# Loads behind the moves of turned tiles, mirroring in two steps, and new tables in a two-layer encoder on one core

## The chip, the core and the metric

The kernel runs on one core of a Trainium2 chip. Five engines take part, each with its own instruction stream: TensorE (PE; its weight loads are listed as PEld) multiplies, VectorE (DVE) and ScalarE (ACT) work on tiles, GpSimd (POOL) does a few small things and issues transfers, and SyncE (SP) does nothing but issue transfers. Two queues of transfers matter: that of SP and that of POOL. The metric is the device time of one execution in microseconds (us), the median of several runs.

## What is computed

The reference is a trunk of two layers over 256 positions of width 2048 with 16 heads, all in float32:

```python
# layer 1
u = rms_norm(h, a_norm_g);  q, k, v, fz = split(u @ a_w_in)     # q, k normalized per head
o = forgetting_attention(q, k, v, log_sigmoid(fz + a_b_f))      # causal, with a cumulative bias
h = h + o @ a_w_out
h = h + (relu(rms_norm(h, g) @ w1) ** 2) @ w2                   # w1: 2048 x 8192, w2: 8192 x 2048
# keys and values for layer 2, once
k_sh, v_sh = split(rms_norm(h, kv_norm_g) @ kv_w)               # k_sh normalized per head
# layer 2
q = rms_norm_heads(rms_norm(h, b_norm_g) @ b_w_q)
o = chunked_relbias_attention(q, k_sh, v_sh, b_rel)
h = h + o @ b_w_out
h = h + (relu(rms_norm(h, g) @ w1) ** 2) @ w2
```

## The kernel before

**Split products.** Each float32 operand is split into a high half, rounded, and a low half, what the rounding left. A product of weights and activations takes three passes: high by high (L628), high weights by low activations (L630), low weights by high activations (L632). The high half of a 128x1024 piece of weights is made by ACT (`hi`, L310), the low half by DVE (`lo`, L319), which needs the high one. There are four buffers for high halves and four for low ones. A *unit* is one such piece and its 12 matmuls on 512 columns (six in a form's half, below).

**The feed-forward.** Its hidden width is worked off in four chunks. A chunk has four *pairs* of products: w10 and w11 (two halves of `x @ w1`) and w20 and w21 (two halves of the second product); in layer 1 the query projection follows as pairs q0 and q1. A pair is computed partly by a fast matrix scheme with seven products, the *forms* f0 to f6, each in two halves, and partly plainly: the plain units are called a and b, after the two accumulators that they add to. A form takes sums of weight blocks. Blocks `11` and `12` of a pair are brought into their own tiles (`bring`, L337, on SP). `12` gets block `22` added by a transfer that accumulates (T3, L350, on POOL); `make` adds `11` on DVE (T2, L357); T4 adds the raw block `21`, which form f4 used, on DVE (L348); T1 adds `12` to `11` by an accumulating transfer (L350). f4's and f6's blocks and all plain units come through three raw buffers (`raw`, loads L293 and L295 on SP); one is free again when its low halves, or T4 for `21`, have been made. Between forms, partial sums are combined: `p7` (ACT) and then L673 and L675 on DVE, after which the next form writes on.

**Turned tiles.** Results must be transposed before the next product. DVE transposes blocks of 32x32 (L475, `z`), and 16 transfers of 32 partitions each, called moves (L490), bring them to their place: every other one is SP's, the rest POOL's. Hidden values are then taken by ACT (relu L990, squares L995 and L997) and DVE (low half L1001); rows of x by ACT (L451, L454) and DVE (L455), and sums of them for the forms by L433 to L442.

**The order.** Instructions of PE, DVE, ACT and SP run in the order in which they are written. What is written when is set by tables. ORDER lists the units of each pair (`r` takes a plain unit left over from the pair before). LOOK says by how many units the low halves are written ahead of the matmuls of a unit, MORE how many high halves beyond that. BEHIND tells after which form half's low half, and how many low halves later, a `bring`, `make` or `add` is written. HIDDEN, LONG, SHORT, AGAIN and QUERY deal the steps of turned tiles (transposes, moves, splitting) out over the following units; these steps stand in a list, `fill`, of which `run_fill` takes one item per unit. In `fetch` (L378), which runs ahead of each unit, low halves, high halves and then raw loads are written: loads go on while fewer than EARLY (4) halves are waiting. `flip` (L611) mirrors the mean squares of the rows for the reversed order in which keys and values are computed: a copy of the mirrored identity on DVE (L614), a matmul (L615), and what follows from it.

Of the kernel before, what the change touches and what calls it, by code (L numbers as in the profile page):

```python
# [9 lines left out]
F32 = mybir.dt.float32  # L10
# [5 lines left out]
P = 128  # L16
# [13 lines left out]
EARLY = 4  # L30
MINI = 0
HIDDEN = (
# [4 lines left out]
)  # L37
UA = UN // 512
LONG = (
# [4 lines left out]
)  # L44
SHORT = (
# [4 lines left out]
)  # L50
REL = 384
QUERY = (0, 1, 13, 10, 5, 9, 3)
AGAIN = (0, 0, 1, 3, 4, 4, 7, 5)
ATT = ((8, 14, 18, 18, 10), (8, 8, 12, 12, 9), (8, 13, 18, 18, 10), (8, 8, 12, 12, 8))
BIAS = ((3, 6, 7), (3, 6, 4))
LOOK = {
# [6 lines left out]
}  # L63
MORE = {
# [6 lines left out]
}  # L71
ORDER = {
# [9 lines left out]
}  # L82
BEHIND = {
    "w10": {(0, 0): [(0, 1, "make", 0), (7, 1, "add", "T1", 0)], (0, 1): [(2, 1, "add", "T1", 1), (0, 1, "make", 1)], (1, 1): [(1, 0, "bring", "12", 0), (0, 0, "bring", "12", 1)], (3, 1): [(6, 0, "bring", "11", 0), (6, 0, "bring", "11", 1)], (4, 0): [(1, 1, "add", "T4", 0)], (4, 1): [(0, 1, "add", "T4", 1), (9, 0, "add", "T3", 1)], (6, 0): [(0, 0, "add", "T3", 0)]},
    "w11": {(0, 0): [(0, 1, "make", 0), (7, 1, "add", "T1", 0)], (0, 1): [(2, 1, "add", "T1", 1), (0, 1, "make", 1)], (1, 1): [(1, 0, "bring", "12", 0), (1, 0, "bring", "12", 1)], (3, 1): [(5, 0, "bring", "11", 0)], (4, 0): [(0, 1, "add", "T4", 0)], (4, 1): [(0, 1, "add", "T4", 1), (9, 0, "add", "T3", 1)], (6, 0): [(1, 0, "add", "T3", 0)], (2, 1): [(7, 0, "bring", "11", 1)]},
    "w20": {(0, 0): [(7, 1, "add", "T1", 0), (0, 1, "make", 0)], (0, 1): [(0, 1, "make", 1)], (1, 1): [(0, 0, "bring", "12", 0), (1, 0, "bring", "12", 1), (3, 1, "add", "T1", 1)], (3, 1): [(5, 0, "bring", "11", 0), (2, 0, "bring", "11", 1)], (4, 0): [(2, 1, "add", "T4", 0)], (4, 1): [(0, 1, "add", "T4", 1), (8, 0, "add", "T3", 1)], (6, 0): [(0, 0, "add", "T3", 0)]},
    "w21": {(0, 0): [(0, 1, "make", 0), (6, 1, "add", "T1", 0)], (0, 1): [(0, 1, "make", 1), (0, 1, "add", "T1", 1)], (1, 1): [(2, 0, "bring", "12", 1)], (3, 1): [(5, 0, "bring", "11", 0)], (4, 0): [(1, 1, "add", "T4", 0)], (4, 1): [(0, 1, "add", "T4", 1), (9, 0, "add", "T3", 1), (5, 0, "bring", "11", 1)], (6, 0): [(1, 0, "add", "T3", 0)], (2, 1): [(1, 0, "bring", "12", 0)]},
    "q0": {(0, 0): [(0, 1, "make", 0), (7, 1, "add", "T1", 0)], (0, 1): [(3, 1, "add", "T1", 1), (0, 1, "make", 1)], (1, 1): [(0, 0, "bring", "12", 0), (1, 0, "bring", "12", 1)], (3, 1): [(5, 0, "bring", "11", 0), (3, 0, "bring", "11", 1)], (4, 0): [(1, 1, "add", "T4", 0), (0, 0, "add", "T3", 0)], (4, 1): [(0, 1, "add", "T4", 1), (10, 0, "add", "T3", 1)]},
    "q1": {(0, 0): [(0, 1, "make", 0), (9, 1, "add", "T1", 0)], (0, 1): [(5, 1, "add", "T1", 1), (0, 1, "make", 1)], (1, 1): [(1, 0, "bring", "12", 1)], (3, 1): [(7, 0, "bring", "11", 1), (4, 0, "bring", "11", 0)], (4, 0): [(1, 1, "add", "T4", 0)], (4, 1): [(0, 1, "add", "T4", 1), (9, 0, "add", "T3", 1)], (6, 0): [(0, 0, "add", "T3", 0)], (2, 1): [(1, 0, "bring", "12", 0)]},
}  # L90
SUBS = {"1": (2, 2), "2": (2, 2), "q": (2, 2)}
OPENING = (
    (18, "bring", "12", 0),
    (19, "bring", "12", 1),
    (9, "add", "T3", 0),
    (5, "add", "T3", 1),
    (4, "bring", "11", 0),
    (14, "bring", "11", 1),
)
BIG = 2 * UN  # L100
FORMS = ("11", "T3", "T2", "T1", "21", "T4", "22")
# [14 lines left out]
def trunk(ctx: ExitStack, tc: tile.TileContext, t):  # L116
# [19 lines left out]
    ps_o = pool("ps_o", 2, space=PSUM)  # L136
# [24 lines left out]
    first = sm.tile([P, GH], F32, name="first", bufs=1)  # L161
# [216 lines left out]
    def fetch(ahead=AHEAD, early=EARLY, more=0):  # L378
        while (units or raws or highs) and len(ready) <= ahead:
            low()  # L380
        while (units or raws) and len(ready) + len(highs) <= ahead + more and can_high():
            high()
        while units and sum(r[3] for r in raws) < early:
            load()
        return ready.popleft()

    fill = deque()

    def run_fill():
        if fill:  # L390
            for f in fill.popleft():
                f()
# [178 lines left out]
    class RowStats:  # L571
# [37 lines left out]
            yield  # L609

        def flip(self):  # L611
            pm = ps_o.tile([P, 512], F32, name="pt", tag="po")
            flipper = wk.tile([P, P], F32, name="flipper", tag="wk")
            V.tensor_copy(flipper, ident[:, ::-1])  # L614
            TE.matmul(pm[:, :NB], flipper, self.ms, start=True, stop=True)  # L615
# [369 lines left out]
    def mlp(plan, x, Sx, st, last, query=None):  # L985
# [49 lines left out]
        for it in plan:  # L1035
            p = it.pair
            if isinstance(p, Pair):
                n = it.u if it.kind == "f" else 7
                hl = fetch(LOOK[p.key][n], more=MORE[p.key][n])
            else:  # L1040
                hl = fetch()
            assert it.u < 4 or it.kind == "f" or it.u * 2 < len(p.x or range(99)), (p.stage, p.n, it.u, len(p.x))
            if p.ps is None:
                open_pair(p)
                if not p.prev:
                    for ps in (p.ps[1][0], p.ps[0][1]):
                        TE.matmul(ps, p.x[0][:, 0, :P], hl[0][:, :512], start=True, stop=True)
            if it.kind == "f":
                form_products(p, *hl, it.u, it.s)
            else:  # L1050
                products(p.ps[it.kind], *hl, p.x, it.u, not units and not ready, isinstance(p, Pair))
            if it.kind != "f" or it.s == p.subs - 1:
                run_fill()
                q = {"f4": 0, "f5": 0, "f6": 1}.get(f"f{it.u}") if it.kind == "f" else it.kind
                if q is not None:
                    p.left[q] -= 1
                    if not p.left[q]:
                        for b in range(NB):
                            p.evac[q](b, p.ps[q][b])
# [147 lines left out]
```

## Time and profile before

| | |
|---|---|
| median of three runs | 2105.89 us (2103.67 to 2107.0) |
| the profiled execution | 2103.45 us |
| its span | 2101.7 us |
| matmuls busy (PE) | 2069.0 us, 98% |
| VectorE busy | 1723.8 us, 82% |
| ScalarE busy | 1290.3 us, 61% |
| GpSimd busy | 354.8 us, 17% |
| mean transfer rate | 256 GB/s, 538.89 MB in all |

The profile is of one execution. Busy times of PE have modelled ends, so a matmul of 512 columns is shown as 0.39 us where the next starts after 0.23. In a row of the timeline stand the start, the time, engine, line, operation, tiles and how many are taken together; in brackets the idle time before it and what ended it. The feed-forward of layer 1 lies at about 393 to 1130 us with the query pairs at its end, the keys, values and attention of layer 2 up to about 1430, the feed-forward of layer 2 from there to the end.

### The profile page before, as it was taken

The page shows a single profiled execution, that of the slowest core. Times are in us where ns is not written, and L with a number is a line of the kernel's source. Part 1 is how long each engine was busy: PE and PEld are TensorE (multiplying, and loading weights), DVE is VectorE, ACT ScalarE, POOL GpSimd, SP SyncE. Part 2 cuts the span into 40 slices and gives each one's busy share as a digit, 9 for nine tenths or more (in the row PEclk, how much of TensorE's full clock was granted, in tenths as well). Part 3 has the DMA queues.
Part 4 walks back from the last instruction along what each step waited for, and adds up shares of the span by engine and source line. Part 5 has one row for each costly group of instructions (what it writes and reads, how often), then busy time and mean ns, then how long its engine had stood idle before and what let it go on. Part 6 is the DMA issues. An engine that isn't in the chain of part 4 may idle for free. (4 is left out here: it accounts for less than half of the span.)

```text
span 2101.7 us, 26998 instructions
## 1 busy us (share of the span) xinstructions
PE 2069.0 (98%) x9114; PEld 1696.5 (81%) x9114; DVE 1723.8 (82%) x2003; ACT 1290.3 (61%) x1567; POOL 354.8 (17%) x552
## 2 busy tenths in 40 slices
PE   9999999999999999999999999999999999999999
PEld 7888888787887887887777888887878878878877
DVE  6777676898888889888999576768988998898896
ACT  6544545776667567567777444456765765675674
POOL 1001001231032022022224000022310310220220
PEclk9999999999999999999999999999999999999999
DMA  8777778899898898899886777688997988988884
GB/s 304 242 254 225 238 245 277 259 254 274 258 285 244 250 297 246 264 267 282 251 252 202 260 238 239 226 276 254 265 282 251 271 258 262 286 255 258 267 270 167
DMA packets 160635, 538.89 MB, mean 256 GB/s; under 512 B 42848, under 2 KB 68080, under 8 KB 125680
## 3 DMA queue, kind: packets, MB, share of 16 engines
q1 hardware_dynamic: 129136, 453.78, 60.8%
q0 software_dynamic: 31360, 83.39, 21.4%
q8 instruction: 71, 1.16, 0.2%
q14 instruction: 68, 0.56, 0.1%
HBM read 497.20 MB, written 15.75 MB: 244 GB/s over the span
## 5 line engine op out<-in xcount | busy, mean ns | idle before, releaser
L319 DVE TENSOR_TENSOR lo<-raw,hi 128x1024 fp32r<-128x1024 f32 (+1 forms) x634 | 753.4, 1213 | 149.7 <-ACT hi L310 137.4
L310 ACT ACTIVATE hi<-raw 128x1024 fp32r<-128x1024 f32 (+1 forms) x634 | 651.0, 1052 | 330.0 <-PE acc L630 129.6
L628 PE MATMUL acc<-hi,act 128*128 128x512 f32 x1644 | 456.1, 394 | 5.6 <-ACT hi L310 2.0
L632 PE MATMUL acc<-lo,act 128*128 128x512 f32 x1644 | 449.0, 390 | 1.7 <-DVE lo L319 1.7
L630 PE MATMUL acc<-hi,act 128*128 128x512 f32 x1644 | 448.8, 389 | 0.0
L628 PEld LDWEIGHTS acc<-hi,act 128*128 128x128 f32 x1644 | 306.8, 188 | 71.1 <-ACT hi L310 3.6
L632 PEld LDWEIGHTS acc<-lo,act 128*128 128x128 f32 x1644 | 307.9, 188 | 68.4 <-DVE lo L319 4.3
L630 PEld LDWEIGHTS acc<-hi,act 128*128 128x128 f32 x1644 | 308.5, 188 | 65.2 <-DVE act L421 0.5
L319 DVE TENSOR_TENSOR lo<-w,hi 128x1024 fp32r<-128x1024 f32 x204 | 243.8, 1214 | 18.6 <-ACT hi L310 18.4
L310 ACT ACTIVATE hi<-w 128x1024 fp32r<-128x1024 f32 x204 | 211.3, 1053 | 73.3 <-PE po L630 29.8
L490 POOL DMA_DIRECT2D q<-z x336 | 170.3, 517 | 259.1 <-DVE z L475 95.0
L310 ACT ACTIVATE hi<-wT 128x1024 fp32r<-128x1024 f32 x136 | 140.8, 1054 | 77.4 <-DVE wT L348 48.5
L319 DVE TENSOR_TENSOR lo<-wT,hi 128x1024 fp32r<-128x1024 f32 x136 | 160.3, 1216 | 4.8 <-ACT hi L310 3.7
L628 PE MATMUL s<-hi,act 128*128 128x512 f32 x476 | 136.7, 391 | 4.5 <-ACT hi L310 2.8
L632 PE MATMUL s<-lo,act 128*128 128x512 f32 x476 | 137.0, 392 | 0.6 <-DVE lo L319 0.5
L630 PE MATMUL s<-hi,act 128*128 128x512 f32 x476 | 136.0, 390 | 0.0
L628 PEld LDWEIGHTS s<-hi,act 128*128 128x128 f32 x476 | 89.0, 188 | 25.2 <-ACT hi L310 4.1
L632 PEld LDWEIGHTS s<-lo,act 128*128 128x128 f32 x476 | 88.5, 188 | 22.8 <-DVE lo L319 4.8
L630 PEld LDWEIGHTS s<-hi,act 128*128 128x128 f32 x476 | 88.7, 188 | 19.7 <-DVE act L1001 1.4
L727 POOL TENSOR_TENSOR rn<-vv,mhalf 128x4 f32<-128x4 f32 x32 | 44.4, 1401 | 336.3 <-DVE vv L726 336.2
L350 POOL DMA_DIRECT2D w<-in_f1a x32 | 28.6, 967 | 320.4 <-ACT hi L310 191.2
L357 DVE TENSOR_TENSOR wT<-w,w 128x1024 f32<-128x1024 f32 x68 | 82.7, 1217 | 0.0
(183 smaller groups left out, 2333.4 us busy)
## 6 DMA issues: line engine op xcount, KB each, us to landing
raw<-in_w_in SPq DMA_DIRECT2D x94, 512.0 KB, 5.3
raw<-in_s1a SPq DMA_DIRECT2D x32, 1024.0 KB, 6.8
raw<-in_s2a SPq DMA_DIRECT2D x32, 1024.0 KB, 6.7
raw<-in_w_kv SPq DMA_DIRECT2D x64, 512.0 KB, 5.6
raw<-in_s1b SPq DMA_DIRECT2D x32, 1024.0 KB, 6.7
raw<-in_s2b SPq DMA_DIRECT2D x32, 1024.0 KB, 5.7
raw<-in_w_oa SPq DMA_DIRECT2D x32, 512.0 KB, 5.6
w<-in_f1a SPq DMA_DIRECT2D x16, 1024.0 KB, 6.7
```

The costliest lines, as they stand in the source:

```text
L310: S.activation(hi[:, c], raw[:, c], AF.Copy)
L319: V.tensor_tensor(lo[:, c], raw[:, c], hi[:, c].bitcast(F32), op=ALU.subtract)
L350: G.dma_start(d, p.big[block][:, half(s)], accum_op=ALU.add)
L357: V.tensor_tensor(p.t["T2"][:, half(s)], p.t["T3"][:, half(s)], p.t["11"][:, half(s)], op=ALU.add)
L490: (SY, G)[j % 2].dma_start(d[32 * j : 32 * j + 32, i], z[32 * i : 32 * i + 32, j * n : (j + 1) * n])
L628: TE.matmul(ps, xh, cut(hi, j), start=first, stop=False, **kw)
L630: TE.matmul(ps, xl, cut(hi, j), start=False, stop=False, **kw)
L632: TE.matmul(ps, xh, cut(lo, j), start=False, stop=last, **kw)
L727: G.tensor_tensor(rn, vv, mhalf, op=ALU.pow)
```

## The change

Raw loads are no longer written in `fetch` ahead of a unit's matmuls but in a function of their own, `top_up`, which the loop over the feed-forward's plan calls after the unit's matmuls and its step of `fill`. The loops of the other stages load as before. `flip` yields after the copy and again at its end, and its two parts stand in `fill` two items apart. All tables that set the order have new numbers, with a few rows left as they were.

```diff
@@ tables (a few lines of each)
 HIDDEN = (
     (3, 3, 3, 5, 8, 9, 9, 10, 11, 12),
-    (0, 2, 3, 3, 5, 7, 7, 7, 9, 9),
-    (1, 1, 3, 3, 5, 5, 8, 9),
-    (1, 3, 4, 4, 7, 8, 9, 9),
+    (0, 2, 2, 2, 5, 6, 7, 7, 9, 9),
+    (0, 2, 2, 2, 5, 5, 8, 9),
+    (0, 3, 4, 4, 7, 8, 9, 9),
 )
...
-    (8, 0, 1, 2, 2, 3, 4, 4),
+    (7, 0, 0, 0, 1, 2, 4, 4),
...
-    "q0": (2, 2, 2, 2, 1, 2, 1, 2),
+    "q0": (2, 2, 1, 2, 1, 2, 2, 2),
...
-    "w20": "r f0 r f1 f2 f4 r f3 f5 a r r a b f6 r",
+    "w20": "r f0 f1 r f2 f4 r r f3 f5 a a r r b r f6 r",
...
@@ in fetch
         while (units or raws) and len(ready) + len(highs) <= ahead + more and can_high():
             high()
+        if early:
+            top_up(early)
+        return ready.popleft()
+
+    def top_up(early=EARLY):
         while units and sum(r[3] for r in raws) < early:
             load()
-        return ready.popleft()
@@ flip
         def flip(self):
-            pm = ps_o.tile([P, 512], F32, name="pt", tag="po")
             flipper = wk.tile([P, P], F32, name="flipper", tag="wk")
             V.tensor_copy(flipper, ident[:, ::-1])
+            yield
+            pm = ps_o.tile([P, 512], F32, name="pt", tag="po")
             TE.matmul(pm[:, :NB], flipper, self.ms, start=True, stop=True)
...
             self.flipped = f
+            yield
@@ the loop over the plan, and where flip is put
-                hl = fetch(LOOK[p.key][n], more=MORE[p.key][n])
+                hl = fetch(LOOK[p.key][n], 0, MORE[p.key][n])
...
             if it.kind != "f" or it.s == p.subs - 1:
                 run_fill()
+            top_up()
+            if it.kind != "f" or it.s == p.subs - 1:
                 q = {"f4": 0, "f5": 0, "f6": 1}.get(f"f{it.u}") if it.kind == "f" else it.kind
...
-                    add_fill([[]] * QUERY[6] + [[st2.flip]])
+                    step = steps(st2.flip)
+                    add_fill([[]] * QUERY[6] + [[step], [], [step]])
```

The code after is a few lines longer, so lines move: L475 becomes L479, L490 L494, L673 L679, L675 L681, L1001 L1007. Three places show what the new order does.

SP's queue in the first chunk of layer 1, from pair w21's block `12` (in_f2a, the first w tile) to its block `11` (the second) and the raw load behind it; the raw in_f2a between is form f6's of w20, q<-z are moves of hidden tiles. Before:

```order
L337 DMA w_4168<-in_f2a 128x2048
L295 DMA raw<-in_s2a 128x2048
L490 DMA q<-z 32x256 x2
L295 DMA raw<-in_f2a 128x2048
L490 DMA q<-z 32x256 x6
L337 DMA w_4323<-in_f2a 128x2048
L295 DMA raw<-in_s2a 128x2048
```

After:

```order
L337 DMA w_4176<-in_f2a 128x2048
L295 DMA raw<-in_s2a 128x2048
L494 DMA q<-z 32x256 x4
L295 DMA raw<-in_f2a 128x2048
L337 DMA w_4316<-in_f2a 128x2048
L494 DMA q<-z 32x256 x4
L295 DMA raw<-in_s2a 128x2048
```

Block `11` now stands directly behind f6's raw load, with four moves behind it instead of six in front; two more moves stand ahead of the raw load.

DVE in the same place, from the transposes in pair w20 to the low halves of w21's f2 (w_3963 is w20's block `11`, w_4168 and w_4323 are w21's `12` and `11`, wT_4090 is T2 or T4 of w20, wT_4381 T2 of w21). Before:

```order
L475 STREAM_TRANSPOSE z<-acc 128x4x4x32 x2
L319 TENSOR_TENSOR lo<-wT_4090,hi 128x1024 x2
L319 TENSOR_TENSOR lo<-raw,hi 128x1024 x2
L348 TENSOR_TENSOR wT_4090<-wT_4090,raw 128x1024
L673 TENSOR_TENSOR s<-p_4211,po 128x512
L319 TENSOR_TENSOR lo<-w_3963,hi 128x1024
L348 TENSOR_TENSOR wT_4090<-wT_4090,raw 128x1024
...
L319 TENSOR_TENSOR lo<-w_4168,hi 128x1024 x2
L1001 TENSOR_TENSOR act<-q,act 128x1024
L319 TENSOR_TENSOR lo<-wT_4381,hi 128x1024 x2
```

After (w_3945, w_4176, wT_4086 and wT_4379 are the same tiles):

```order
L319 TENSOR_TENSOR lo<-wT_4086,hi 128x1024 x2
L479 STREAM_TRANSPOSE z<-acc 128x4x4x32 x2
L319 TENSOR_TENSOR lo<-raw,hi 128x1024
L348 TENSOR_TENSOR wT_4086<-wT_4086,raw 128x1024
L319 TENSOR_TENSOR lo<-raw,hi 128x1024
L348 TENSOR_TENSOR wT_4086<-wT_4086,raw 128x1024
L679 TENSOR_TENSOR s<-p_4186,po 128x512
L319 TENSOR_TENSOR lo<-w_3945,hi 128x1024 x2
...
L319 TENSOR_TENSOR lo<-w_4176,hi 128x1024 x2
L319 TENSOR_TENSOR lo<-wT_4379,hi 128x1024 x2
L1007 TENSOR_TENSOR act<-q,act 128x1024
```

The transposes stand behind f2's low halves, both T4 additions ahead of L679 and of f3's low halves, and L1007 behind the low halves of w21's f2.

DVE in the query pair q0, around the partial sum that its form f3 waits for (w_8749 and w_8751 are its block `11`, from which f3's two low halves are made). Before:

```order
L475 STREAM_TRANSPOSE z<-h_91 128x4x4x32
L319 TENSOR_TENSOR lo<-w_8749,hi 128x1024 x2
L673 TENSOR_TENSOR s<-p_8965,po 128x512
L319 TENSOR_TENSOR lo<-raw,hi 128x1024 x2
L348 TENSOR_TENSOR wT_8813<-wT_8813,raw 128x1024 x2
```

After:

```order
L479 STREAM_TRANSPOSE z<-h_91 128x4x4x32
L319 TENSOR_TENSOR lo<-w_8751,hi 128x1024
L679 TENSOR_TENSOR s<-p_8961,po 128x512
L319 TENSOR_TENSOR lo<-w_8751,hi 128x1024
L319 TENSOR_TENSOR lo<-raw,hi 128x1024 x2
L348 TENSOR_TENSOR wT_8809<-wT_8809,raw 128x1024 x2
```

L679 stands one low half earlier than L673 did.

More of the change, by code (lines that the diff above doesn't have):

```diff
@@ L39 @@
 LONG = (
[4 rows of a table removed]
[4 rows of a table added]
 )
 SHORT = (
[4 rows of a table removed]
[4 rows of a table added]
 )
 REL = 384
-QUERY = (0, 1, 13, 10, 5, 9, 3)
-AGAIN = (0, 0, 1, 3, 4, 4, 7, 5)
+QUERY = (0, 1, 13, 11, 9, 10, 3)
+AGAIN = (0, 0, 1, 2, 4, 3, 6, 5)
 ATT = ((8, 14, 18, 18, 10), (8, 8, 12, 12, 9), (8, 13, 18, 18, 10), (8, 8, 12, 12, 8))
-BIAS = ((3, 6, 7), (3, 6, 4))
+BIAS = ((3, 6, 7), (8, 6, 3))
 LOOK = {
[6 rows of a table removed]
[6 rows of a table added]
 }
 MORE = {
[6 rows of a table removed]
[6 rows of a table added]
 }
 ORDER = {
[9 rows of a table removed]
[9 rows of a table added]
 }
 BEHIND = {
[L84 to L89, printed above, removed]
@@ new lines @@
+    "w10": {(0, 0): [(0, 1, "make", 0), (8, 1, "add", "T1", 0)], (0, 1): [(2, 1, "add", "T1", 1), (1, 1, "make", 1)], (1, 1): [(1, 0, "bring", "12", 0), (1, 0, "bring", "12", 1)], (3, 1): [(7, 0, "bring", "11", 0), (4, 0, "bring", "11", 1)], (4, 0): [(0, 1, "add", "T4", 0)], (4, 1): [(0, 1, "add", "T4", 1), (9, 0, "add", "T3", 1)], (5, 0): [(1, 0, "add", "T3", 0)]},
+    "w11": {(0, 0): [(0, 1, "make", 0), (6, 1, "add", "T1", 0)], (0, 1): [(3, 1, "add", "T1", 1), (0, 1, "make", 1), (3, 0, "bring", "12", 0)], (3, 1): [(3, 0, "bring", "11", 0)], (4, 0): [(1, 1, "add", "T4", 0)], (4, 1): [(0, 1, "add", "T4", 1), (7, 0, "add", "T3", 1)], (6, 0): [(1, 0, "add", "T3", 0)], (2, 1): [(7, 0, "bring", "11", 1), (2, 0, "bring", "12", 1)]},
@@ new lines @@
+    "w20": {(0, 0): [(7, 1, "add", "T1", 0), (0, 1, "make", 0)], (0, 1): [(0, 1, "make", 1)], (1, 1): [(1, 0, "bring", "12", 0), (4, 1, "add", "T1", 1), (0, 0, "bring", "12", 1)], (3, 1): [(5, 0, "bring", "11", 0), (1, 0, "bring", "11", 1)], (4, 0): [(0, 1, "add", "T4", 0)], (4, 1): [(0, 1, "add", "T4", 1), (7, 0, "add", "T3", 1)], (6, 0): [(0, 0, "add", "T3", 0)]},
+    "w21": {(0, 0): [(0, 1, "make", 0), (7, 1, "add", "T1", 0)], (0, 1): [(0, 1, "make", 1), (0, 1, "add", "T1", 1)], (3, 1): [(5, 0, "bring", "11", 0)], (4, 0): [(0, 1, "add", "T4", 0)], (4, 1): [(0, 1, "add", "T4", 1), (9, 0, "add", "T3", 1), (5, 0, "bring", "11", 1)], (6, 0): [(0, 0, "add", "T3", 0)], (2, 1): [(0, 0, "bring", "12", 0), (2, 0, "bring", "12", 1)]},
@@ new lines @@
+    "q0": {(0, 0): [(7, 1, "add", "T1", 0), (0, 1, "make", 0)], (0, 1): [(4, 1, "add", "T1", 1), (1, 1, "make", 1)], (1, 1): [(1, 0, "bring", "12", 0), (2, 0, "bring", "12", 1)], (3, 1): [(5, 0, "bring", "11", 0), (3, 0, "bring", "11", 1)], (4, 0): [(1, 1, "add", "T4", 0), (0, 0, "add", "T3", 0)], (4, 1): [(0, 1, "add", "T4", 1), (11, 0, "add", "T3", 1)]},
+    "q1": {(0, 0): [(0, 1, "make", 0), (7, 1, "add", "T1", 0)], (0, 1): [(4, 1, "add", "T1", 1), (1, 1, "make", 1)], (1, 1): [(2, 0, "bring", "12", 1)], (3, 1): [(7, 0, "bring", "11", 1), (3, 0, "bring", "11", 0)], (4, 0): [(1, 1, "add", "T4", 0)], (4, 1): [(0, 1, "add", "T4", 1), (9, 0, "add", "T3", 1)], (6, 0): [(0, 0, "add", "T3", 0)], (2, 1): [(3, 0, "bring", "12", 0)]},
@@ L93 @@
     (18, "bring", "12", 0),
-    (19, "bring", "12", 1),
-    (9, "add", "T3", 0),
-    (5, "add", "T3", 1),
+    (17, "bring", "12", 1),
+    (7, "add", "T3", 0),
+    (11, "add", "T3", 1),
     (4, "bring", "11", 0),
-    (14, "bring", "11", 1),
+    (8, "bring", "11", 1),
 )
```

52 rows, old and new, of tables (LONG, LOOK, MORE, ORDER) are left out of this document.

## The prediction

> **What bounds the kernel now.** First the page: span, then the share of each engine.
>
> ```profile
> span 2101.7 us, 26998 instructions
> ...
> PE 2069.0 (98%) x9114; PEld 1696.5 (81%) x9114; DVE 1723.8 (82%) x2003; ACT 1290.3 (61%) x1567; POOL 354.8 (17%) x552
> ```
>
> TensorE is the bound. Since the change leaves its matmuls as they are, only the gaps between them can be won. Next the windows, which show where the gaps are (the columns after the window are its width, then PE, PEld, DVE, ACT and POOL busy, the granted clock, DMA share and GB/s):
>
> ```profile
> 1000.00:1100.00 100.00, 95.44 (x409) 77.13 (x408) 94.08 (x102) 72.79 (x99) 24.27 (x42) 0.98 0.87 253
> ...
> 1200.00:1400.00 200.00, 200.00 (x916) 167.01 (x915) 138.29 (x238) 94.29 (x158) 18.94 (x27) 1.00 0.74 237
> ```
>
> The attention stages have none; the feed-forward has them. Then the timeline of TensorE in one chunk of layer 1 (chunk 2, pairs w20 and w21):
>
> ```profile
> 824.93 1.07 PE L628 MATMUL po<-hi,act 128*128 128x512 f32 x4
> 825.84 1.07 PE L630 MATMUL po<-hi,act 128*128 128x512 f32 x4
> ...
> 835.07 0.73 PE L632 MATMUL acc<-lo,Sh 128*128 128x512 f32 x2 [0.61 <-DVE lo L319]
> ...
> 838.48 0.73 PE L632 MATMUL acc<-lo,Sh 128*128 128x512 f32 x2 [0.40 <-DVE lo L319]
> ```
>
> Four unstalled matmuls take 825.84 - 824.93 = 0.91 us, 226.5 ns each. Busy times include a modelled end, so I count stalls as width less matmuls times 226.5 ns. Every chunk has the same two places: w20's forms f3, f5 and the two units after them (48 matmuls), and w21's forms f0, f1, f2 (36 matmuls; 60 in the last chunk of a layer, where two other units lie between). First rows and sums over the eight chunks, for w20 and then w21:
>
> ```profile
> 479.07:491.10 12.03, 11.51 (x50) 8.77 (x48) 10.41 (x10) 4.85 (x5) 1.73 (x2) 1.00 0.88 222
> ...
> sum 96.53, PE 92.30 PEld 70.19 DVE 83.61 ACT 41.23 POOL 13.71; mean PE 11.54 PEld 8.77 DVE 10.45 ACT 5.15 POOL 1.71
> ```
>
> ```profile
> 496.54:507.21 10.67, 9.08 (x37) 6.47 (x36) 10.67 (x10) 9.81 (x12) 1.71 (x2) 1.00 0.92 230
> ...
> sum 90.63, PE 82.10 PEld 61.32 DVE 89.88 ACT 80.53 POOL 13.69; mean PE 10.26 PEld 7.67 DVE 11.23 ACT 10.07 POOL 1.71
> ```
>
> w20: 96.53 - 384 x 0.2265 = 9.6 us. w21: 90.63 - 336 x 0.2265 = 14.5 us. Together 24 us in a kernel with, by the page, 2101.7 - 2069.0 = 33 us without a matmul. In both places PE waits for DVE's low halves (lo L319). What DVE itself waits for differs. The same chunk, DVE, then ACT, then the SP queue:
>
> ```profile
> 813.47 1.21 DVE L348 TENSOR_TENSOR wT<-wT,raw 128x1024 f32<-128x1024 f32 x1
> ...
> 824.98 2.36 DVE L319 TENSOR_TENSOR lo<-raw,hi 128x1024 fp32r<-128x1024 f32 x2 [1.59 <-ACT hi L310]
> 829.25 1.23 DVE L319 TENSOR_TENSOR lo<-w,hi 128x1024 fp32r<-128x1024 f32 x1 [1.91 <-ACT hi L310]
> ...
> 836.07 1.22 DVE L1001 TENSOR_TENSOR act<-q,act 128x1024 fp32r<-128x1024 f32 x1
> ```
>
> ```profile
> 823.89 2.01 ACT L310 ACTIVATE hi<-raw 128x1024 fp32r<-128x1024 f32 x2 [4.23 <-DMA raw<-in_f2a]
> ...
> 828.16 2.01 ACT L310 ACTIVATE hi<-w 128x1024 fp32r<-128x1024 f32 x2 [0.31 <-DMA w<-in_f2a]
> ```
>
> ```profile
> 814.76 0.33 SPq L295 DMA_DIRECT2D raw<-in_f2a  x1
> 815.14 4.42 SPq L490 DMA_DIRECT2D q<-z  x6
> 819.73 0.47 SPq L337 DMA_DIRECT2D w<-in_f2a  x1
> ```
>
> At w20 DVE has no wait up to 824.98; it is simply full. At w21 it is late because it idled 1.59 + 1.91 = 3.5 us for two transfers: form f6's raw block, issued at 814.76 right behind the second T4 addition (L348), and w21's block w11, issued at 819.73 behind six moves.
>
> **The change part by part.**
>
> *The w20 to w21 crossing.* On DVE both T4 additions of w20 now stand ahead of L679 (old L673; 0.69 us in its row for q0 below) and of the first low half of f3 (2.36 / 2 = 1.2 us, by the rows above), 1.7 us when instructions overlap a little. The transposes, which now come behind f2's two low halves, may wait, though: they used to start at 804.86, so they would start 2.32 later, at 807.2, and the unit that they read ends now where f2's second half used to start, at 807.47.
>
> ```profile
> 804.86 1.30 DVE L475 STREAM_TRANSPOSE z<-acc 128x512 f32<-128x512 f32 x2
> 806.10 2.32 DVE L319 TENSOR_TENSOR lo<-wT,hi 128x1024 fp32r<-128x1024 f32 x2
> ```
>
> ```profile
> 807.47 0.62 PE L628 MATMUL po<-hi,Sh 128*128 128x512 f32 x2
> ```
>
> With the last matmul's drain that is a wait of 0.3 to 0.5, say 0.4 us, so f6's load goes out about 1.7 - 0.4 = 1.3 us earlier. On SP, w11 now stands ahead of the last four moves; it needs f3's low halves, finished at about 816 (the T4 row's 813.47 and two operations of 1.2), and so goes out some 3.4 us earlier. Whether earlier issue is earlier landing is for the DMA engines to say:
>
> ```profile
> 814.00:816.00 2.00, 1.48 (x7) 0.88 (x7) 1.93 (x3) 1.20 (x2) 1.39 (x2) 1.00 0.46 70
> ...
> 826.00:828.00 2.00, 2.00 (x10) 1.65 (x10) 1.34 (x2) 1.06 (x1) 0.00 (x0) 1.00 1.03 426
> ```
>
> They are half empty when f6 is issued and full later. I credit f6 with all 1.3 us, and w11 with 1.5 of its 3.4 (lower end 0, if the engines hand the whole gain back). DVE then starts w21's low halves 1.3 to 1.6 us earlier. Besides, L1007 (old L1001) moves from ahead of f2's low halves to behind them: 1.14 us more for f2 alone. Stalls of 14.5 / 8 = 1.8 us a chunk meet 1.3 to 1.6 us for f1 and 2.4 to 2.7 for f2; what stays is about 0.3 a chunk, 2.4 in all. Term: -12.1, between 0 and -14.5.
>
> *w20 itself.* The same DVE work stands ahead of f3 and the two units, so the 9.6 us stay; the transposes' wait ends up in it. I take a third of its 0.4 us, 0.15 a chunk: +1.2, between 0 and +3.2. On POOL one T3 accumulation now goes ahead of the eight moves, for which I put nothing: POOL is 17% busy, and the moves' reader, the relu on ACT, now stands two high halves later.
>
> *The query pair q0.* PE, DVE and the granted clock:
>
> ```profile
> 1062.56 0.61 PE L632 MATMUL po<-lo,S 128*128 128x512 f32 x2
> 1066.11 0.83 PE L628 MATMUL po<-hi,S 128*128 128x512 f32 x2 [2.93 <-DVE s L673]
> ...
> 1070.51 0.62 PE L628 MATMUL s<-hi,act 128*128 128x512 f32 x2
> ```
>
> ```profile
> 1063.04 2.31 DVE L319 TENSOR_TENSOR lo<-w,hi 128x1024 fp32r<-128x1024 f32 x2
> 1065.27 0.69 DVE L673 TENSOR_TENSOR s<-p,po 128x512 f32<-128x512 f32 x1
> ```
>
> ```profile
> 1066.00:1070.00 4.00, 3.90 (x10) 3.11 (x11) 4.00 (x4) 3.97 (x10) 4.00 (x8) 0.57 0.88 198
> ```
>
> PE stands from 1063.01 (1062.56 and two matmuls) to 1066.11, 3.1 us, because f3 overwrites what L673 must read and L673 stands behind f3's two low halves. After that the clock is 0.57: twelve matmuls take 1070.51 - 1066.11 = 4.4 instead of 2.7 us, 1.7 more. In the new order L679 stands one low half earlier (2.31 / 2 = 1.15 us), so the stall is 2.0 us. I take the slow clock as gone with it, because the stall of 1.9 us that ends at 1147.01 (below) leaves the clock at 1.00 in the next 3.4 us:
>
> ```profile
> 1147.40:1150.80 3.40, 3.40 (x17) 2.81 (x16) 3.33 (x7) 1.90 (x2) 2.12 (x2) 1.00 0.87 287
> ```
>
> Term: -1.1 - 1.7 = -2.8, between -1.1 and -4.8. The Trainium skill (TensorE: Matmul & The Clock Gate, Part 1: The HAM clock gate) says that the clock halves after an idle window of about 3.4 us. The trace differs a little: here 3.1 us were enough; by the rule 2.0 us cost no clock and the term is -2.8, by a lower limit that the row leaves possible it is -1.1.
>
> *Flip in two steps, and the first K/V group.*
>
> ```profile
> 1129.81 0.35 PE L615 MATMUL pt<-msb,flipper 128*128 128x2 f32 x2 [0.87 <-DVE flipper L614]
> ...
> 1147.01 0.73 PE L628 MATMUL acc<-hi,act 128*128 128x512 f32 x2 [1.66 <-DVE qn L731]
> ```
>
> With two units between copy and matmul, the 0.87 us wait goes: -0.9 (0 if the copy slips as far). At 1147 L455 no longer stands between the first K/V low halves and qn (an operation on 128x1024, as L1001's 1.22 us), but its ACT part now precedes the squares: I take half, -0.6, between +1 and -1.7.
>
> *The openings.* At the start of each feed-forward, f5 waits for a high half that stands behind the splitting of turned x:
>
> ```profile
> 1456.43 0.73 PE L628 MATMUL s<-hi,act 128*128 128x512 f32 x2 [1.56 <-ACT hi L310]
> ```
>
> ```profile
> 1452.64 1.71 ACT L451 ACTIVATE y<-q,gsb 128x256 f32<-128x256 f32 x4 [2.51 <-DMA q<-z]
> ```
>
> The moves that L451 waits for now go out one unit's steps earlier in SHORT's last row, and without a raw load between. The transposes ahead of them come no earlier, so I take a part of the 2.51 us only, 0.55, twice (layers 1 and 2): -1.1, between +2 and -3.
>
> Elsewhere a raw load now stands behind the same unit's moves. I put nothing for that: the next row has raw loads waiting 479 us for a buffer, so most are issued as soon as a buffer is free and are early; the cover is the third raw buffer.
>
> ```profile
> SPq L295 <- DVE lo L319: 478.8, 134, 12.8
> ...
> SPq L490 <- DVE z L475: 52.7, 19, 10.2
> ...
> ACT hi L310 <- DMA raw<-in_f2b: 24.0, 6, 5.7
> ```
>
> Sum: -12.1 + 1.2 - 2.8 - 0.9 - 0.6 - 1.1 = -16.3 us. Against the profiled execution (2103.45 us, span 2101.7 and 1.75 around it) that is 2087.1; it ran 2.4 below the median of 2105.89, so the median comes to 2089.6: 2089.
>
> **The rivals.**
>
> *Moves in front of loads (slower).* A move waits for its transposes (L490's row: 2.8 us on average, 10.2 at most) and takes 4.42 / 6 = 0.74 us to issue, and now raw loads queue behind it. Four moves and an average wait make a load 5.8 us later. ACT's row above has loads that are already late, 24.0 us in six waits. If one load a chunk has only 3.5 us to spare, that is 2.3 x 8 = 18 us, and with the other terms (-4.2) and w21's gain kept the sum is about +2; if it is a load in front of w21, its gain is lost as well: +14, 2120. The middle is 2114. It decides as soon as a load is later than its margin; against it speak the 479 us. The Trainium skill (DMA: Bandwidth & Descriptors, Queues, rings and completion order) speaks for it: each DMA engine takes a ring's descriptors in order, so a load behind moves also starts behind their data. No row here shows the order within a ring.
>
> *Nothing won at w21.* The DMA engines are full from 816 us on, w11 lands as late as before, or DVE, which was full for w20, only shifts its stall from w21 to the units behind it. Then -4.2 us of the other terms stay: 2101.7, at the edge of no change. For it: the share of 1.03. Against: DVE's 3.5 us of idle time are real, and f6's load starts with the engines half empty.
>
> *More than costed.* w20's stall shrinks too, since the new order asks for lead time earlier, and the openings reach their bounds: -16.3 - 9 = 2080.
>
> **Chances.** Forecast 0.60 (its own range 2083 to 2097), loads late 0.14, nothing won 0.14, more won 0.12. The range leaves out the late loads and some of the far end: 2078 to 2106. What this kernel's measurement tells from no change is 0.2%, 4.2 us. Faster: 0.60 + 0.12 + 0.06 of the third case = 0.78; same 0.08; slower 0.14.
>
> **What will show it.** Right: no DVE idle time over 2 us in front of w21's f0, PE without waits of 0.4 us or more in w21's f1 and f2, w20's waits as before; a stall of 2 us in front of q0's f3 and a clock of 1.00 behind it; no wait for the flipper. Wrong: new rows of ACT waiting for raw blocks, above all where eight moves stand together; or a w20 stall that grows by what w21's loses.

## The result and the profile after

The changed kernel takes 2088.43 us (median of four runs, 2085.9 to 2090.83), the kernel before 2106.43 in the runs beside it: a ratio of 0.9917 (95% interval 0.9899 to 0.9935). Forecast were 2089 us and a gain of 0.8%. The profiled execution is one of the longer ones, 2090.83 us; its page:

```profile
span 2089.0 us, 27013 instructions
...
PE 2064.4 (99%) x9114; PEld 1697.4 (81%) x9114; DVE 1724.3 (83%) x2003; ACT 1297.5 (62%) x1567; POOL 354.3 (17%) x552
```

So the span of this execution is 12.7 us shorter than that of the profiled one of before, and by the medians the gain is 18.0. The work of DVE and ACT is nearly the same; waits are fewer. The two places in each chunk, first the windows of w21's f0 to f2 (last row and sum), then w20 (sum; here the windows begin with f4, so 60 matmuls each, because the wait has moved in front of f3):

```profile
2030.07:2043.87 13.80, 13.80 (x61) 11.19 (x60) 12.11 (x12) 9.53 (x12) 1.69 (x2) 1.00 0.71 188
sum 78.61, PE 77.39 PEld 61.58 DVE 65.83 ACT 63.49 POOL 9.98; mean PE 9.67 PEld 7.70 DVE 8.23 ACT 7.94 POOL 1.25
```

```profile
sum 118.49, PE 112.29 PEld 88.85 DVE 118.49 ACT 76.68 POOL 38.40; mean PE 14.04 PEld 11.11 DVE 14.81 ACT 9.59 POOL 4.80
```

w21: 78.61 - 336 x 0.2265 = 2.5 us, 12.0 less than before. w20: 118.49 - 480 x 0.2265 = 9.8 us, against 9.6 before (which the same 60 matmuls a chunk also give there). DVE is busy all the time in these windows (118.49 of 118.49).

The crossing in chunk 2 of layer 1, SP's queue, ACT and DVE:

```profile
810.77 0.33 SPq L295 DMA_DIRECT2D raw<-in_f2a  x1
813.59 0.33 SPq L337 DMA_DIRECT2D w<-in_f2a  x1
813.98 2.93 SPq L494 DMA_DIRECT2D q<-z  x4
819.87 0.33 SPq L295 DMA_DIRECT2D raw<-in_s2a  x1
```

```profile
822.83 1.06 ACT L310 ACTIVATE hi<-w 128x1024 fp32r<-128x1024 f32 x1 [1.73 <-PE s L638]
...
825.59 1.04 ACT L996 ACTIVATE q<-q 128x1024 f32<-128x1024 f32 x1
```

```profile
823.93 1.23 DVE L319 TENSOR_TENSOR lo<-w,hi 128x1024 fp32r<-128x1024 f32 x1 [0.68 <-ACT hi L310]
```

Block 11 goes out directly behind f6's raw load, and DVE waits 0.68 us in front of w21's first low half instead of 1.91. ACT's first high half of it now waits for a buffer that PE frees (L638), not for a transfer. The four moves go out at 813.98, and the relu that needs them, L996, does not wait at all.

In q0 the wait in front of f3 is shorter, but the half clock is still there. PE's timeline, then a window behind the wait:

```profile
1062.11 1.06 PE L634 MATMUL po<-hi,S 128*128 128x512 f32 x2 [1.87 <-DVE s L679]
```

```profile
1062.30:1065.60 3.30, 3.30 (x9) 2.52 (x9) 3.30 (x4) 3.27 (x6) 2.83 (x6) 0.50 0.88 273
```

### The profile page after: what moved, and what is told of

The parts are those of the page before. It is cut to its first block, busy times and chain, and to the rows that moved or that the text cites. A ratio compares the mean times of both kernels' runs of the same rounds, so it can differ in the third digit from the quotient of the medians.

```text
span 2089.0 us, 27013 instructions
## 1 busy us (share of the span) xinstructions
PE 2064.4 (99%) x9114; PEld 1697.4 (81%) x9114; DVE 1724.3 (83%) x2003; ACT 1297.5 (62%) x1567; POOL 354.3 (17%) x552
## 4 chain that ended last, share of the span: by engine, by line
PE 87%; DVE 6%; DMA 3%; issue 2%; ACT 2%; SPq 0%; ACTq 0%; DVEq 0%; POOL 0%
PE acc L634 19%; PE acc L636 19%; PE acc L638 18%; PE po L634 5%; PE po L638 5%; PE po L636 5%; PE s L636 5%; PE s L638 5%; PE s L634 4%; DVE lo L319 3%; ACT hi L310 1%; DMA w<-in_f2a 1%; PE s L792 1%; PE po L823 1%; DVE wT L348 1%
## 5 line engine op out<-in xcount | busy, mean ns | idle before, releaser
L310 ACT ACTIVATE hi<-raw 128x1024 fp32r<-128x1024 f32 (+1 forms) x634 | 655.1, 1053 | 320.3 <-PE acc L636 130.9
L638 PE MATMUL acc<-lo,act 128*128 128x512 f32 x1644 | 449.2, 390 | 1.9 <-DVE lo L319 1.8
L638 PEld LDWEIGHTS acc<-lo,act 128*128 128x128 f32 x1644 | 308.0, 188 | 68.8 <-DVE lo L319 4.7
L310 ACT ACTIVATE hi<-w 128x1024 fp32r<-128x1024 f32 x204 | 211.5, 1055 | 100.1 <-PE po L636 30.6
L494 POOL DMA_DIRECT2D q<-z x336 | 170.3, 519 | 234.3 <-DVE z L479 82.0
L310 ACT ACTIVATE hi<-wT 128x1024 fp32r<-128x1024 f32 x136 | 140.9, 1053 | 54.1 <-DVE wT L348 26.5
L638 PE MATMUL s<-lo,act 128*128 128x512 f32 x476 | 136.1, 390 | 0.6 <-DVE lo L319 0.5
L638 PEld LDWEIGHTS s<-lo,act 128*128 128x128 f32 x476 | 89.0, 188 | 20.9 <-DVE lo L319 2.6
```

The source lines that it names most:

```text
L310: S.activation(hi[:, c], raw[:, c], AF.Copy)
L494: (SY, G)[j % 2].dma_start(d[32 * j : 32 * j + 32, i], z[32 * i : 32 * i + 32, j * n : (j + 1) * n])
L638: TE.matmul(ps, xh, cut(lo, j), start=False, stop=last, **kw)
```

## The experiments

My theory after the result: what stands where around the w20 to w21 crossing (block 11 early, L1007 behind f2) gives most of the gain, and the position of the raw loads as such costs and gives little. The rival: the position of the loads is the cause. "Waits" below are always widths less matmuls times 226.5 ns, in the profiled execution; where the clock is at half, the longer matmuls count in them too (about 1.7 us for each 3.4 us at half).

**1. The changed kernel again.**

> The changed kernel once more, since its four runs came in two pairs, near 2086 and near 2091 us. If the pairs are two outcomes of the free position of the clock's window against the wait in q0 (about 2 us), a profiled execution near 2086 should show a granted clock of 1.00 behind that wait, 1.7 us less there, and other small differences. If the pairs have another cause, the clock dips in both. Either way 2085 to 2091.

2091.3 us, ratio 0.9929 (0.9914 to 0.9944), just above what was expected. w21 waits 0.6 us in all here, w20 9.9. The clock dips to half behind q0's wait here too, with a time of 2088.98. No profiled execution fell near 2086, so what separates the lower runs from the higher ones stays open.

**2. The new tables, with raw loads back ahead of the moves.**

```diff
-                hl = fetch(LOOK[p.key][n], 0, MORE[p.key][n])
+                hl = fetch(LOOK[p.key][n], more=MORE[p.key][n])
...
-            top_up()
-            if it.kind != "f" or it.s == p.subs - 1:
```

> The changed kernel with its raw loads back ahead of the unit's moves; tables and flip new. Theory (tables carry the gain): within 4 us of the changed kernel, 2088 to 2092, w21's waits still under 4 us in all. Rival (loads behind moves carry it): 2098 or more, with w21's waits back.

2107.17 us, ratio 1.0004 (0.9990 to 1.0018): the whole gain is gone, and my theory as it stood with it. Counted from the starts of the matmuls, w21 waits 9.4 us here, against 2.5 and 0.6 in the changed kernel's two profiles, and the openings (f4 to f5) 9.9 against 0.6 and 0.3. The crossing in chunk 2, SP's queue, DVE, ACT and PE:

```profile
818.50 0.33 SPq L337 DMA_DIRECT2D w<-in_f2a  x1
824.77 0.33 SPq L295 DMA_DIRECT2D raw<-in_s2a  x1
825.15 2.41 SPq L494 DMA_DIRECT2D q<-z  x4
```

```profile
816.12 2.35 DVE L319 TENSOR_TENSOR lo<-w,hi 128x1024 fp32r<-128x1024 f32 x2
```

```profile
834.35 1.07 ACT L996 ACTIVATE q<-q 128x1024 f32<-128x1024 f32 x1 [3.73 <-DMA q<-z]
```

```profile
836.41 0.73 PE L634 MATMUL acc<-hi,Sh 128*128 128x512 f32 x2 [0.55 <-ACT hi L310]
```

Block 11 was out at 818.5, 2.4 us behind the start of f3's low halves on DVE (816.12), as in the changed kernel, whose row for these is:

```profile
811.21 2.35 DVE L319 TENSOR_TENSOR lo<-w,hi 128x1024 fp32r<-128x1024 f32 x2
```

But four moves stand behind a raw load that waits for a free buffer: they go out 9.0 us behind that start, where the changed kernel issues them 2.8 us behind it. They land at about 834, 18.0 us behind that start against 14.0 in the changed kernel; L996 waits 3.73 us for them, and the high halves of w21's f1 stand behind L996 on ACT. What ACT waited for moves in all, first here, then in the changed kernel:

```profile
ACT y L455 <- DMA q<-z: 21.2, 8, 4.6
ACT q L996 <- DMA q<-z: 20.9, 8, 3.7
```

```profile
ACT y L455 <- DMA q<-z: 2.6, 4, 1.0
...
ACT q L996 <- DMA q<-z: 0.8, 2, 0.4
```

**3. Pair w20's tables alone, on the kernel before** (its rows of LOOK, MORE, ORDER and BEHIND).

```diff
-    "w20": "r f0 r f1 f2 f4 r f3 f5 a r r a b f6 r",
+    "w20": "r f0 f1 r f2 f4 r r f3 f5 a a r r b r f6 r",
```

> The kernel before with the new LOOK, MORE, ORDER and BEHIND rows of pair w20 alone; loads stay ahead of the moves, flip and all else as before. On SP, w21's block 11 then has two moves instead of six in front, on DVE both T4 additions stand ahead of f3's low halves, and L1001 stands behind w21's f2. Theory (the crossing is won by what stands where in w20): w21's waits fall from 14.5 us to under 3, w20's grow by 0.2 a chunk, so about -11 in all, 2095 +-3. Rival (it is the position of the raw loads that wins): no more than -3, 2103 or more.

2105.28 us, ratio 0.9995 (0.9985 to 1.0005). w21's waits go from 14.5 to 12.3 us only, though block 11 is early and L1001 behind f2. ACT:

```profile
ACT q L990 <- DMA q<-z: 16.0, 6, 3.6
```

Before, this row was:

```profile
ACT q L990 <- DMA q<-z: 1.9, 3, 0.9
```

The wait for block 11 was replaced by one for the moves.

**4. The position of the loads alone, on the kernel before.** The edit is `top_up` and its call, without any table.

> The kernel before with raw loads behind the moves of their unit and nothing else. Two of the six moves ahead of w21's block 11 go ahead of f6's raw load, which waits anyway, so block 11 goes out 1.5 us earlier. Theory: w21's waits shrink by a third to a half, 5 us in all, L1001 is still in front of f2; about 2101 +-4. Rival (position of the loads is the cause of the whole gain): 2092 or less. Rival (loads late behind moves): over 2108, with new waits of ACT for raw blocks.

2104.49 us, ratio 0.9985 (0.9975 to 0.9996). w21 waits 13.9 us, half a us less than before. So neither of these two parts gives more than 2 us by itself; the gain is in the order and the position of the loads together.

**5. Loads ahead of the moves in pair w20 only.**

```diff
-                hl = fetch(LOOK[p.key][n], 0, MORE[p.key][n])
+                hl = fetch(LOOK[p.key][n], EARLY * (p.key == "w20"), MORE[p.key][n])
```

> The changed kernel with raw loads ahead of the moves in pair w20 alone; all engines but SP keep their order. At the crossing, four moves then stand behind a raw load that waits for a free buffer. Theory (a move behind such a load goes out some 10 us later, and ACT's relu L996, which waits for it, holds up the high halves of w21's f1 and f2): w21 waits 1 to 1.5 us a chunk, 6 to 10 us in all. Rival (the position of the loads matters elsewhere only): within 2 us of the changed kernel.

2096.41 us, ratio 0.9955 (0.9938 to 0.9971), that is 5 to 8 us more than the changed kernel's two medians. w21 waits 8.3 us, 5.8 more than in the changed kernel's first profile and 7.7 more than in its second, as expected, and ACT waits for moves again:

```profile
ACT q L996 <- DMA q<-z: 15.2, 5, 3.5
```

**6. Loads ahead of the moves in the opening pair only.** In each layer, one raw load goes ahead of the last two of eight moves on SP; PE, DVE and ACT keep their order.

```diff
-                hl = fetch(LOOK[p.key][n], 0, MORE[p.key][n])
+                hl = fetch(LOOK[p.key][n], EARLY * (not p.prev), MORE[p.key][n])
```

> The changed kernel with raw loads ahead of the moves in the first pair of each feed-forward alone: one raw load goes ahead of the last two of eight moves, twice in the kernel. Theory as before: those two moves wait with the load for a buffer, ACT's splitting of turned x (L455) waits for them, f5's high halves stand behind it: 4 us in layer 1, 5 in layer 2, 9 in all. Rival (two moves are worth 1 to 2 us at most): under 4 in all.

2098.34 us, ratio 0.9968 (0.9956 to 0.9979). The waits from f4 to f5 in the openings are 3.8 and 3.7 us instead of 0.2 and 0.4, so 7 of the expected 9; in layer 1, 1.7 us of it is the half clock that followed the wait. With run 5, this reproduces the loss of run 2: 5 to 8 us from pair w20 and 7 to 10 from the openings, of 16 to 19. The size came out nearly right, but not by the expected way. SP's queue and ACT here, in layer 1:

```profile
395.16 3.68 SPq L494 DMA_DIRECT2D q<-z  x6
398.95 0.52 SPq L295 DMA_DIRECT2D raw<-in_s1a  x1
399.52 1.14 SPq L494 DMA_DIRECT2D q<-z  x2
```

```profile
405.50 1.71 ACT L455 ACTIVATE y<-q,gsb 128x256 f32<-128x256 f32 x4 [3.32 <-DMA q<-z]
```

and in the changed kernel, where all eight moves go first:

```profile
395.17 4.98 SPq L494 DMA_DIRECT2D q<-z  x8
400.26 2.66 SPq L295 DMA_DIRECT2D raw<-in_s1a  x2
```

```profile
403.01 1.71 ACT L455 ACTIVATE y<-q,gsb 128x256 f32<-128x256 f32 x4 [0.83 <-DMA q<-z]
```

The load hardly waits for a buffer, and the two moves are issued only half a us later; yet their reader starts 2.5 us later. One load is 1 MB, and at the 442 GB/s of the next window it is 2.4 us of transfer:

```profile
402.00:403.00 1.00, 1.00 (x6) 0.81 (x6) 1.00 (x2) 0.18 (x1) 0.00 (x0) 1.00 1.04 442
```

So the moves' bytes come behind the load's. The Trainium skill (DMA: Bandwidth & Descriptors, Queues, rings and completion order) has the rule, that each DMA engine consumes the descriptors of one ring in order. SP's two moves fit it in sign and in size. But the rule is about one ring, and the trace shows that the delay isn't bound to SP's queue. POOL's last two moves here were issued just ahead of the load and just behind it, at 398.77 and 399.26:

```profile
L494 POOL DMA_DIRECT2D q<-z x2: 496/497/498, 398.8 to 399.3; - x2
DMA to landing us min/median/max: 1.7/3.6/5.4
```

The earlier one landed after 1.7 us, the later one after 5.4, like SP's two (5.3 and 4.9; in the changed kernel 3.3 and 2.8). The load of 1 MB held up what was issued behind it on either queue.

**7. The old LONG and SHORT in the changed kernel.**

```diff
-    (7, 0, 0, 0, 1, 2, 4, 4),
+    (8, 0, 1, 2, 2, 3, 4, 4),
```

and the other rows of both tables likewise.

> The changed kernel with the old LONG and SHORT, which deal out the turning of x. Theory (the openings gain by loads behind moves and by these tables together): the waits in front of f5 come back in part, 1 to 4 us in all, half of what the changed kernel gained there. Rival (the tables alone carry the openings): 4 us or more, as before the change. Rival (the position of the loads alone does): under 1.

2099.05 us, ratio 0.9962 (0.9949 to 0.9974). The openings wait 4.3 and 5.2 us, above what I expected and more than before the change (1.4 and 2.4); 1.7 us of each is the half clock that followed the wait. w21 waits 7.8 us here, against 2.5 and 0.6, so the time is not lost in the openings alone. The tables and the position of the loads are not halves of a gain in the openings either: either one undone, all of it is gone.

**8. Block 11 behind the moves again.**

```diff
-(3, 1): [(5, 0, "bring", "11", 0), (1, 0, "bring", "11", 1)]
+(3, 1): [(6, 0, "bring", "11", 0), (0, 0, "bring", "11", 1)]
```

> The changed kernel with w21's block 11 brought one low half later, which puts it behind the four moves and the raw load that it stood ahead of (on SP some 6.5 us later). Theory of the prediction (early issue of block 11 carries most of the gain at the crossing): w21's f0 waits for it, 2 to 3.5 us a chunk, 16 to 28 us in all, 2106 to 2118. Rival (block 11 is early enough anyway, the gain is in the moves that no longer stand behind a load): within 4 us of the changed kernel.

2115.99 us, ratio 1.0043 (1.0029 to 1.0056), slower than the kernel before. w21 waits 16.1 us. SP's queue and ACT:

```profile
825.96 0.37 SPq L337 DMA_DIRECT2D w<-in_f2a  x1
```

```profile
832.91 2.01 ACT L310 ACTIVATE hi<-w 128x1024 fp32r<-128x1024 f32 x2 [5.96 <-DMA w<-in_f2a]
```

So the early block 11 is needed, as the prediction had it. The price is higher than that of the old place, because it isn't the moves alone that it stands behind now:

```profile
816.79 2.85 SPq L494 DMA_DIRECT2D q<-z  x4
825.51 0.33 SPq L295 DMA_DIRECT2D raw<-in_s2a  x1
```

The moves were out at 819.6; the raw load in front of block 11 waited for a buffer until 825.51, and block 11 with it.

**9. L1007 ahead of f2's low halves.**

```diff
-    (0, 3, 4, 4, 7, 8, 9, 9),
+    (0, 3, 4, 4, 7, 8, 8, 8),
```

> The changed kernel with L1007 (once a chunk, in w21) back ahead of f2's low halves, where L1001 stood. Theory of the prediction (its move gives 1.1 us to f2): f2 waits 0.7 us or more in every chunk, 5 to 9 us in all. Rival (with block 11 early DVE has enough lead, L1007's place is worth nothing): within 2 us of the changed kernel.

2098.23 us, ratio 0.9955 (0.9939 to 0.9971), 7 to 10 us above the changed kernel. w21 waits 14.3 us, 1.79 in nearly every chunk. The relu's squares on ACT come a step earlier with it, so the edit moves L1003 as well, and the run does not part the two.

**10. L679 in q0 ahead of both low halves.**

```diff
-    "q0": (2, 2, 1, 2, 1, 2, 2, 2),
+    "q0": (2, 2, 0, 2, 1, 2, 2, 2),
```

> The changed kernel with LOOK of q0's f2 at 0 instead of 1, so that L679 stands ahead of both low halves of f3 in q0. Theory (the wait in front of f3 and the half clock behind it hang on L679's place, and the clock falls when most of one window of 3.4 us is idle): the wait falls from 2.0 to about 0.9 us and the clock stays at 1.00 behind it, 1.1 + 1.7 = 2.8 us less than the changed kernel, unless f3's own low halves are now late (up to 1 us of it back). Rival (the clock falls there for another reason): 1.1 us less at most, with a clock of 0.5 for 3.4 us as before.

2088.55 us, ratio 0.9914 (0.9896 to 0.9932): the same as the changed kernel within the intervals. PE and the window behind the wait:

```profile
1057.17 0.70 PE L634 MATMUL po<-hi,S 128*128 128x512 f32 x2 [0.95 <-DVE s L679]
1065.62 1.19 PE L636 MATMUL s<-hi,act 128*128 128x512 f32 x4 [1.57 <-DVE act L459]
```

```profile
1057.20:1060.60 3.40, 3.40 (x14) 2.60 (x15) 3.40 (x4) 3.40 (x7) 1.98 (x4) 1.00 0.62 178
```

The wait fell and the clock stayed full, as expected, and nothing came of it: three units on, PE now waits 1.57 us for L459, DVE's low half of turned x. From f2 to the plain units q0 waits 3.6 us in all here, 3.7 in the changed kernel, 4.8 before. DVE is what q0 is bound by; the slow clock fell for the most part into time that would have been waited anyway. In run 5, q0's wait was the same 1.88 us as in the changed kernel and the clock stayed full behind it; PE then waited 0.69 us for L459 instead, and q0 3.4 us in all:

```profile
1061.08 0.70 PE L634 MATMUL po<-hi,S 128*128 128x512 f32 x2 [1.88 <-DVE s L679]
```

```profile
1061.10:1064.50 3.40, 3.40 (x15) 2.83 (x16) 3.40 (x4) 3.37 (x7) 3.40 (x8) 1.00 0.69 231
```

**11. Flip in two steps and q0's sum, on the kernel before** (the edit of `flip` and of its place in `fill`, and LOOK of q0's f2 at 1).

> The kernel before with flip in two steps and LOOK of q0's f2 at 1 instead of 2, nothing else. Theory: the wait for the flipper goes, 0.9 to 1.0 us; the wait in front of q0's f3 falls from 3.1 to 2.0 us, but by what the run with L679 still earlier showed the next plain units then wait for L459 instead, so q0 as a whole gains no more than 1 us. 1 to 2 us in all. Rival (the terms of the prediction add up): 3.7 us.

2107.06 us, ratio 0.9995 (0.9983 to 1.0006). The wait for the flipper is gone, but PE stands longer at the end of q1 and the first K/V unit:

```profile
1146.12 0.70 PE L630 MATMUL acc<-hi,act 128*128 128x512 f32 x2 [1.49 <-ACT sq L721]
1148.49 1.22 PE L630 MATMUL acc<-hi,act 128*128 128x512 f32 x2 [1.66 <-DVE qn L733]
```

By itself the flip moved most of its wait one stage on. From the flipper's matmul to the first K/V group the time beyond 226.5 ns a matmul is 6.1 us here, 3.9 before and 1.1 in the changed kernel. Of the 6.1, some 2.4 are matmuls at half clock behind the two waits above, which there were not before.

**12. Loads ahead of the moves, and all moves issued by POOL.**

```diff
-                (SY, G)[j % 2].dma_start(d[32 * j : 32 * j + 32, i], z[32 * i : 32 * i + 32, j * n : (j + 1) * n])
+                G.dma_start(d[32 * j : 32 * j + 32, i], z[32 * i : 32 * i + 32, j * n : (j + 1) * n])
```

> The kernel with the new tables and raw loads ahead of the moves once more, but with all moves issued by POOL, so that none can stand behind a load on SP. Theory (the loss came from moves that waited in SP's queue behind a raw load that waits for a free buffer, which held up ACT's relu and the high halves behind it): ACT's waits of L996 for moves fall from 21 us to under 5, and the time comes most of the way back, 2090 to 2098. Rival (the loads' data in the DMA engines hold up the moves, whichever queue issues them): L996 still waits, 2104 or more. POOL's additions by transfer come some 4 us later for it, which can cost up to 4 us.

2211.12 us, ratio 1.0489 (1.0469 to 1.0508). It was meant to part the queue on SP from the data in the DMA engines, and it does not: POOL itself became the queue.

```profile
L494 POOL DMA_DIRECT2D q<-z x672 | 336.8, 529 | 275.0 <-DVE z L479 103.6 <-DMA q<-z 69.3 <-DMA w<-in_f2b 25.1
```

A move costs POOL 529 ns of issue, sixteen for each tile stand one behind the other, and L996 waited 46.2 us for them. Inconclusive. The rows of runs 2 and 6 show the two instead: moves issued 6.3 us later in the one, half a us later but landing 2.6 us later in the other, where a move on POOL's queue was held up as well. By these rows a second queue would spare the moves the wait for a free buffer, but not that for the load's data.

None of these kernels is better than the changed one by more than the intervals.

## Why the prediction was right or wrong

The forecast time, 2089, and the direction hold. The terms, against the changed kernel's first profile:

| term | forecast us | measured us |
|---|---|---|
| w21's f0 to f2 | -12.1 | -12.0 (-13.9 in run 1) |
| w20, f3 to the plain units | +1.2 | +0.2 |
| q0, f2 to the plain units | -2.8 | -1.1 |
| flip and first K/V group | -1.5 | -2.8 |
| openings, f4 to f5 | -1.1 | -3.2 |
| other places in w20 and w21 | 0 | +3.7 and +3.0 |

Each is counted from the starts of the matmuls, as the time beyond 226.5 ns each. The sum is -12.2 of the 12.7 us; the rest was not looked for.

*The crossing.* Size and place were right, and runs 8 and 9 show that block 11's early issue and L1007's place are both needed, with 25 to 28 and 7 to 10 us. The step that failed is the sentence on the loads elsewhere: I put nothing for raw loads behind moves, and read SP's 479 us of waits for buffers as cover. They are the opposite. Whatever stands behind a load in SP's queue waits with it, and in the old position those were the moves. Run 2 shows this price, some 16 to 19 us; in the profiles 7 of it lie in w21 and 9 in the openings. Runs 3 and 4 show that w20's tables alone and the position of the loads alone are worth next to nothing. Run 8's 25 to 28 us are more than the old place of block 11 cost, since there it also stands behind a waiting load. I quoted the row of ACT's L310 for raw blocks and looked there for late loads; the row to watch was ACT's relu waiting for moves.

*w20.* Right: the wait stayed, in front of f3 now instead of behind its first half, since DVE has no spare time there. What I had not foreseen are small waits at the start of w20 and late in w21 (chunk 1 of layer 1 above all, 1.7 us at f0 and f1), about 6.7 us that the profiled execution gave back.

*q0.* The wait of 2.0 us came out to a tenth. The clock did not: it fell to half behind it in both profiles of the changed kernel, so "I take the slow clock as gone" failed. It hung on chance: behind the same wait the clock stayed at 1.00 in run 5 (the last section shows why). And the 1.7 us were no term at all, because DVE's L459 bounds q0 with or without them (run 10): in run 5, with the full clock, the same stretch is 1.4 us shorter than before and not 2.8. Of the two values that I set against each other, -1.1 was measured.

*Flip, K/V and openings.* All three signs were right, and the sizes were too small by about half or more. In the openings I took a part of one wait for the earlier moves; runs 6 and 7 show that the moves must be early in the tables and free of a load in the queue, and then the whole wait goes. For the flip, run 11 shows that the forecast reason alone (no wait for the copy) gains nothing, since most of the wait moved on to the end of q1 and the first K/V unit; the rest of the new order is needed for it. Which part of it was not tested.

*The rivals.* Late loads behind moves did not decide: ACT's waits for raw blocks, added up over all rows, were 107.8 us before and 97.1 after. Those of the plain units went down, though those for the forms' blocks of in_f2a went up. Before, then after:

```profile
ACT hi L310 <- DMA raw<-in_f2a: 17.5, 5, 6.3
...
ACT hi L310 <- DMA raw<-in_s2a: 13.6, 4, 4.6
ACT hi L310 <- DMA raw<-in_s1b: 13.3, 7, 2.7
```

```profile
ACT hi L310 <- DMA raw<-in_f2a: 26.4, 8, 6.2
...
ACT hi L310 <- DMA raw<-in_s2a: 4.9, 4, 2.5
...
ACT hi L310 <- DMA raw<-in_s1b: 2.8, 3, 1.4
```

With the loads behind the moves on the old tables (run 4) they were 125.4, so loads do come later for it, at a time that hardly differs. That nothing would be won at w21, the second rival, nearly held for each half of the change alone. Ring order, which I cited for the first rival, would there delay loads behind moves; what the runs show is the reverse, small transfers held up behind large ones, and on the other queue too (run 6).

The forecast was thus right by a sum in which errors of both signs of 1 to 7 us cancelled, which was luck, and its largest term was right in size for a cause that was only half of the cause.

## What to carry to other kernels

In a queue that issues in order, a load that waits for a free buffer holds up everything behind it (run 2: moves out 6.3 us later). One of 1 MB also held up the small transfers issued right behind it by about its own transfer time when it hardly waited itself, on another queue too (run 6). So put the small transfers that somebody is about to need ahead of the bulk loads that have time. Where two edits remove two waits of the same chain, test each alone and both: here each alone gave nothing, since the other wait took its place. And a stall on a bounded engine is not a term until you have named what that stretch waits for next.

## What was not expected of the hardware

TensorE's granted clock fell to 0.50 for about 3.4 us behind a wait of 2.0 us (changed kernel) and stayed at 1.00 behind a wait of the same length in the same place (run 5), so the length of one wait does not decide it. The Trainium skill (TensorE: Matmul & The Clock Gate, Part 1: The HAM clock gate) speaks of free-running windows of 3413 ns and of an idle one before the clock halves. The traces agree with the windows: in each profile all changes of the clock lie on one grid with steps of 3.41 us. Here are two neighbouring steps around the wait in q0, first in the changed kernel, where the wait (1060.07 to 1062.11) lies in one step, then in run 5, where the end of a step at 1059.75 divides it (1059.03 to 1061.08):

```profile
1058.85:1062.26 3.41, 1.54 (x8) 0.99 (x7) 3.41 (x6) 3.41 (x8) 0.00 (x0) 1.00 0.50 184
1062.26:1065.67 3.41, 3.41 (x9) 2.63 (x10) 3.41 (x4) 3.38 (x6) 2.90 (x6) 0.50 0.87 268
```

```profile
1056.33:1059.75 3.42, 2.86 (x13) 2.05 (x11) 3.42 (x5) 3.24 (x7) 0.00 (x0) 1.00 0.77 307
1059.75:1063.16 3.41, 2.08 (x9) 1.78 (x10) 3.41 (x5) 3.41 (x6) 2.69 (x5) 1.00 0.32 91
```

But a window need not be idle throughout, though the skill speaks of an idle one. Over the 14 profiles there are 8138 whole steps at full clock (from 100 us on). In 31 of them PE had 2.04 us or more without a matmul, and each of these was followed by half clock; in the others it had 2.02 us at most, and none was. So here the clock halved when PE stood for about 60% of a step, in one wait or in several, and where a wait of 2.0 us fell on the grid was chance. The wait that the prediction took as its proof, at 1147.01, left 1.94 us idle in its step, just below.

The other number is that of an issuer of many small transfers: 529 ns each on POOL, and 105 us more for the kernel when all moves went through it. SP's eight moves in 4.98 us (run 6) are no faster, 0.62 us each; it is the sixteen in one queue that cost.
